# The transfers of five weight sums in one row, two more heap slots, and low halves that let other vector work pass: a hybrid decoder layer on one core

## The chip, the cores and the metric

The kernel runs on one core of one Trainium2 chip. The metric is the time of one execution in microseconds (us) of the device. Below, PE is TensorE (matmuls), DVE is VectorE, ACT is ScalarE, POOL is GpSimd, and SP is the engine that issues most DMA transfers.

## The reference

One decoder layer over 512 tokens of width 1024, in float32:

```python
u = rmsnorm(h, g_mix)
proj = u @ w_in                     # 1024 x 9232: all that follows is cut from it
ro = retention_chunkwise(rq, rk, rv)            # 8 heads, chunks of 128
y_ret = (silu(rgate) * groupnorm(ro)) @ w_ret_br
do = gated_delta_chunkwise(cq, ck, cv, g, beta) # 8 heads: a triangular solve per chunk,
                                                # then a scan over the 4 chunks
y_dn = (rmsnorm(do) * silu(dz)) @ w_dn_br
h = h + (sigmoid(gate_r) * y_ret + sigmoid(gate_d) * y_dn) @ w_o
up = causal_dwconv(rmsnorm(h) @ w_up) + b       # 1024 -> 2 x 2816
h = h + (silu(a) * b) @ w_down
out = rmsnorm(h)
```

## The kernel before

**Exact products from rounded halves.** Each weight block (128 x 1024 float32, 512 KB) is fetched by an SP transfer into a buffer `wraw` (four of them), rounded by ACT into `whi`, and what is left over is computed by DVE as `wlo = wraw - whi` (four buffers of each). PE multiplies three times per block: high by high, high by low, low by high. One task, `weights()` (line 334), does this for one block after the other. Only when it has issued the `wlo` does it let `fetch()` (line 272) issue the load of another block into the freed buffer.

**Seven products in place of eight.** Five square matrices (numbers 0 to 3: the two gates and the two branches; `OUT`: `w_o`) and `w_down` are multiplied by a scheme of seven half-size products. Four of the seven weight operands are sums of quarters of the matrix (`s1` to `s4`). These sums aren't computed by an engine: `presum()` (line 299) issues transfers on POOL's queue from DRAM to DRAM, a plain copy of one quarter (`s<-wm`) and then a transfer that adds another onto it (`s<-wm` or `s<-s`), eight of 1 MB for each of the five matrices. `presums()` (line 322) spaces them by the program's own clock, and ahead of each it puts a tiny ACT copy `tick` and a tiny POOL copy `tock`, so that POOL can't run ahead of the others.

**Stages, in order of time.** Input norm; the fronts of four delta heads and the retention projections (to about 190 us); the triangular solves, the scans of heads 0 to 3 and the fronts of heads 4 to 7, all mixed (to about 340 us); the gates' projections `pz`, the second solve and scans (to about 455 us); matrices 0 to 3 (tile `py`, to about 610 us; as matrix 3 begins, eight SP loads `h<-x` fetch the residual, line 1348); the OUT product (tile `po`, to about 663 us); the MLP's first product (`pa`, `pb`, to 910 us) and `w_down` (`pd`, to the end).

**How the order is set.** `body()` writes the program as generators that give way to each other. A class `Order` keeps a clock: each PE product advances it by a cost, and a task that is due by that clock is resumed between two products. Each engine then executes its own instructions strictly in the order that comes out, and waits where an operand isn't there. So a cost or a due time changes the order of every engine, and an instruction that waits holds up all behind it on its engine.

**The heap.** Nearly all tiles of 128 x 512 float32 (2 KB a partition) share one pool of `HEAP` slots. The allocator gives a new tile a slot whose earlier tile has no later reader in the program. Its first write then waits until that reader is done. In the scan stage head 4's key tiles, `A` and `ktok` (both written by ACT from the transposed keys `pkt`, `k_front`, line 767), thus stand in slots that heads 0 to 3 have used. A small pool holds the rest, among it the solve's scratch tile `xtmp` (`solve`, line 852) and the retention states `rS`.

Of the kernel before, what the change touches and what calls it, by code (L numbers as in the profile page):

```python
# [11 lines left out]
F32 = mybir.dt.float32  # L12
# [7 lines left out]
P = 128  # L20
# [4 lines left out]
H = 8  # L25
# [33 lines left out]
OUT, DOWN = 4, 5  # L59
# [38 lines left out]
class Order:  # L98
# [29 lines left out]
    def spawn(self, gen, after=0.0):  # L128
        self.n += 1
        heapq.heappush(self.tasks, ((self.clock if self.now is None else self.now) + after, self.n, gen))  # L130
# [91 lines left out]
def body(nc, tc, ctx, io):  # L222
    sp = nc.sync
    order = Order()
    spawn, poll, hold = order.spawn, order.poll, order.hold
    vec = Engine(order, "vec", nc.vector, vec_cost)
# [11 lines left out]
    small = mix.enter_context(tc.tile_pool(name="small", bufs=1))  # L238
    late = []

    HEAP, HEAP2, RAWB, WB = 61, 18, 4, 4

    def S(name, dt=F32):
        return heap.tile([P, T], dt, name=name, tag="s", bufs=HEAP)
# [7 lines left out]
    def PS(name):  # L252
        return psp.tile([P, T], F32, name=name, tag="ps")

    def v3(ap, n=4):
        return ap.rearrange("p (n f) -> p n f", n=n)
# [5 lines left out]
    def ck(n, f=P):  # L262
        return slice(n * f, (n + 1) * f)
# [35 lines left out]
    def presum(ss, parts):  # L299

        todo, late = [], []
        for s in ss:
            steps = [(s, name, i, q) for add in (1, 2) for name, *src in SUMS for i in range(parts) for q in (src[add - 1],)]
            steps = [(*x, n >= len(steps) // 2) for n, x in enumerate(steps)]
            todo += steps[:2 * parts] + late + steps[2 * parts:-parts]
            late = steps[-parts:]
        for s, name, i, q, add in todo + late:
            c = ck(i, 512 * INNER[s] // parts)  # L310
            kw = dict(accum_op=ALU.add) if add else {}
            pool.dma_start(sums[s, name][:, c], quarter(s, q)[:, c], max_dma_last_dim=2048, **kw)
            if add and i == parts - 1:
                made.add((s, name))
            yield
# [5 lines left out]
        act.copy(tick, ones[:, :1])  # L321
        pool.tensor_scalar(tock, tick, 1.0, None, ALU.mult)

    def presums(ss, parts, *times):

        todo = presum(ss, parts)
        for start, end, n in times:
            for i in range(n):
                while order.clock < start + (end - start) * i / n:
                    yield 0.5  # L330
                pace()
                if next(todo, 0) == 0:
                    return
                yield

    def weights():
        i = count["split"]
        if i == len(BLOCKS):
            return
        count["split"] += 1  # L340
        while i not in raws:
            yield 0.3
        raw = raws.pop(i)
        n = raw.shape[1]
        hi = wp.tile([P, n], F32R, name="whi", tag="whi", bufs=WB)
        act.copy(hi, raw)
        yield
        lo = wp.tile([P, n], F32R, name="wlo", tag="wlo", bufs=WB)
        vec.tensor_tensor(lo, raw, hi.bitcast(F32), ALU.subtract)
        ready[i] = (hi, lo)  # L350
        yield
        free[0] += 1
        fetch()
# [10 lines left out]
    def used():  # L364
        spawn(weights(), 0.1)
# [380 lines left out]
    GH = 4  # L746
    NS = GH * NT
    NP = 4 * NS
# [8 lines left out]

    spawn(clear(), 30.0)

    spawn(presums(range(3), 1, (110.0, 318.0, 23), (330.0, 330.0, 1)), 30.0)  # L760
    a_dram = [dram.tile([4, GH, NT, 32, 32], F32, name=f"a_dram{g}") for g in range(2)]
    x_dram = [dram.tile([4, GH, NT, 32, 32], F32, name=f"x_dram{g}") for g in range(2)]
    R32 = [ck(b, 32) for b in range(4)]
    heads = [dict(h=h, got=set()) for h in range(H)]
# [91 lines left out]
    def solve(g):  # L856

        group = heads[g * GH:(g + 1) * GH]
        while not all("k" in hd["got"] for hd in group):
            yield 0.3  # L860
        while g > 0 and not all("o" in hd["got"] for hd in heads[(g - 1) * GH:g * GH]):
            yield 0.3
        sa = [heap.tile([P, 32, 16], F32, name=f"sa{i}", tag="s", bufs=HEAP) for i in range(2)]
        adv = a_dram[g].rearrange("b h n i j -> (b h n) i j")
        for i in range(2):
            sp.dma_start(sa[i][:NP], adv[:, :, ck(i, 16)])
        xx = small.tile([P, 32, 32], F32, name="xx", tag="xx", bufs=1)
        tmp = small.tile([P, 32, 32], F32, name="xtmp", tag="xtmp", bufs=1)
        pool.memset(xx[:NP], 0.0)
        pool.memset(xx.rearrange("p a b -> p (a b)")[:NP, ::33], 1.0)  # L870
        yield 8.0
        for j in range(31):
            shp = [NP, j + 1, 31 - j]
            a = sa[j // 16][:NP, j + 1:, j % 16].unsqueeze(1).to_broadcast(shp)
            tv, xv_ = tmp[:NP, :j + 1, j + 1:], xx[:NP, :j + 1, j + 1:]
            vec.tensor_tensor(tv, a, xx[:NP, :j + 1, j:j + 1].to_broadcast(shp), ALU.mult)
            vec.tensor_tensor(xv_, xv_, tv, ALU.subtract)
            yield
        sp.dma_start(x_dram[g].rearrange("b h n i j -> (b h n) (i j)"), xx[:NP].rearrange("p a b -> p (a b)"))
        for b in range(4):  # L880
            sp.dma_start(tt_all[R32[b], :, R32[b]], x_dram[g][b].rearrange("h n j i -> j (h n) i"))
        yield 13.5
        for i, hd in enumerate(group):
            spawn(solve_up(hd, i), i * 4.0)
# [171 lines left out]
    def ret_state(hp):  # L1056
        sts = states[hp] = [None]
        for n in range(NT - 1):
            pk = PS("pkv")[:, :P]
            for e, r in enumerate(E64):  # L1060
                vv = rv[n][hp // 2][:, ck(2 * hp % 4 + e)]
                pe.matmul(pk[r], krot[n][:, hp, r], vv, start=True, stop=True)
            yield
            st = small.tile([P, P], F32, name="rS", tag="rS", bufs=7)
            if n == 0:
                vec.tensor_copy(st, pk)
            else:
                vec.tensor_tensor(st, pk, sts[n], ALU.add)
            yield
            act.activation(st, st, AF.Identity, scale=gch[:, hp:hp + 1])  # L1070
            sts.append(st)
            yield
# [147 lines left out]
                yield gap  # L1220

    def late_sums():
        while "up" not in heads[H - 1]["got"]:
            yield 0.5
        c = order.clock
        yield from presums((3, OUT), 1, (c, c + 125.0, 15), (c + 140.0, c + 140.0, 1))

    for src, raw, x in ((roT, rr_, "r"), (doT, dd, "d")):
        if x == "d":
# [174 lines left out]
    product(1, o_get, HK, [[(full, C[t], True, o_into(t, 0, C[t], ALU.add, True))] for t in range(2)])  # L1404
    product(6, o_get, HK, [[(full, A[t], False, o_into(t, 1, A[t], ALU.subtract, True))] for t in range(2)], tail=2)
    u2 = (u2hi, u2lo)
    spawn(presums((DOWN,), 4, (order.clock, order.clock + 200.0, 32)))


    def ffn_conv(ps, ci):  # L1410
# [11 lines left out]
    f_raw, act_raw, parts = {}, {}, {}  # L1422
# [7 lines left out]
        parts[name, k] = hi, lo  # L1430

    def combine_f(k):
        y, z = S(f"y{k}"), (S2 if k < 9 else S)(f"z{k}")
        combine(f_raw, k, NK, y, z)
        act_raw["T3", k], act_raw["T1", k] = halves(y)
        act_raw["T2", k], act_raw["T4", k] = halves(z)
        act_raw["B21", k], act_raw["B22", k] = halves(f_raw.pop(k + NK))
        del f_raw[k]
# [195 lines left out]
```

## Time and profile before

| | |
|---|---|
| median of 3 runs | 1023.11 us (1022.1 to 1024.28) |
| profiled execution, its time | 1023.75 us |
| profiled execution, its span (first to last instruction) | 1022.0 us |
| PE busy | 992.4 us, 97% |
| DVE busy | 734.0 us, 72% |
| ACT busy | 535.2 us, 52% |
| POOL busy | 166.0 us, 16% |
| granted clock of TensorE, mean | 0.986 |
| moved by DMA | 189.29 MB |

The profiled execution's time is 1.75 us over its span, and 0.64 us over the median. A row of a timeline gives start, duration, engine, line, operation and `out<-in`; in brackets stands how long the engine sat idle before it, and what ended the wait. A row of waits gives the total, the count and the longest. A row of windows gives the length of a stretch, the busy time of PE, weight load (PEld), DVE, ACT and POOL, then the granted clock, the DMA share and GB/s.

### The profile page before, as it was taken

To read this page: it belongs to the slowest core of one execution; us is meant where nothing else is said; L and a number is where in the kernel's file an instruction comes from. 1 tells how busy PE (TensorE), PEld (TensorE's weight loads), DVE (VectorE), ACT (ScalarE), POOL (GpSimd) and SP (SyncE) were. 2 spreads that over 40 slices of the span, in tenths; PEclk is the share of its full clock that TensorE was granted. 3 is DMA by queue.
4 is the path that set the end of the run, shared out by engine and by line. 5 is a ranking of instruction groups with operands and counts; after the bars stand their busy time and mean duration, and the time that the engine had idled before them with its cause. 6 is when DMAs were issued, how large, how long until landed. Compare 5 with 4: busy or idle time off the path is not lost.

```text
span 1022.0 us, 14344 instructions
## 1 busy us (share of the span) xinstructions
PE 992.4 (97%) x5241; PEld 825.0 (81%) x5241; DVE 734.0 (72%) x1372; ACT 535.2 (52%) x1130; POOL 166.0 (16%) x212
## 2 busy tenths in 40 slices
PE   8999999979999999999999979999999999999997
PEld 7888888767778888888888767788888888888886
DVE  5867797545577796667699869966655676778785
ACT  5599222257744523467686455654444343356664
POOL 3021212112323200032211000022112221000001
PEclk8999999998999999999999989999999999999999
DMA  7243559655757754159999964655669999346663
GB/s 261 72 150 117 138 205 210 204 156 111 202 156 178 167 125 124 42 167 267 346 340 268 272 213 133 199 193 197 221 212 206 207 205 223 91 127 190 202 187 122
DMA packets 82230, 189.29 MB, mean 185 GB/s; under 512 B 22704, under 2 KB 31216, under 8 KB 82160
## 3 DMA queue, kind: packets, MB, share of 16 engines
q1 hardware_dynamic: 54640, 123.36, 37.0%
q0 software_dynamic: 27520, 65.02, 28.3%
q8 instruction: 41, 0.67, 0.2%
q14 instruction: 29, 0.24, 0.1%
HBM read 185.17 MB, written 68.19 MB: 248 GB/s over the span
## 4 chain that ended last, share of the span: by engine, by line
PE 84%; DVE 8%; DMA 3%; issue 2%; ACT 2%; POOL 0%; SPq 0%; POOLq 0%; ACTq 0%; DVEq 0%
PE pa L215 12%; PE pb L215 12%; PE pd L215 10%; PE py L215 9%; PE pz L215 9%; PE pr L215 9%; PE pk L215 5%; PE pv L215 4%; PE pq L215 4%; PE psc L215 3%; DVE wlo L200 2%; DVE res L200 2%; PE pm L215 2%; PE po L215 1%; PE pro L215 1%
## 5 line engine op out<-in xcount | busy, mean ns | idle before, releaser
L200 DVE TENSOR_TENSOR wlo<-wraw,whi 128x1024 fp32r<-128x1024 f32 x212 | 254.6, 1202 | 70.7 <-ACT whi L200 67.8
L200 ACT CAST whi<-wraw 128x1024 fp32r<-128x1024 f32 x212 | 219.0, 1035 | 163.4 <-PE pr L215 60.8
L200 POOL TENSOR_SCALAR tock<-tick 128x1 f32<-128x1 f32 x72 | 31.4, 436 | 461.5 <-ACT tick L200 461.4
L200 DVE SCALAR_TENSOR_TENSOR acc<-pb,prm,acc 128x511 f32<-128x511 f32 (+1 forms) x44 | 33.0, 750 | 57.1 <-ACT acc L200 56.4
L215 PE MATMUL pa<-u2hi,whi 128*128 128x512 f32 (+1 forms) x192 | 72.1, 375 | 1.1 <-ACT u2hi L200 1.1
L215 PE MATMUL pa<-u2lo,whi 128*128 128x512 f32 (+1 forms) x192 | 72.1, 376 | 0.8 <-DVE u2lo L200 0.8
L215 PE MATMUL pa<-u2hi,wlo 128*128 128x512 f32 (+1 forms) x192 | 71.9, 375 | 0.0
L215 PE MATMUL pb<-u2hi,whi 128*128 128x512 f32 (+1 forms) x184 | 70.0, 381 | 0.0
L215 PE MATMUL pb<-u2lo,whi 128*128 128x512 f32 (+1 forms) x184 | 69.9, 380 | 0.0
L215 PE MATMUL pb<-u2hi,wlo 128*128 128x512 f32 (+1 forms) x184 | 69.9, 380 | 0.0
L215 PE MATMUL py<-whi,oh 128*128 128x512 f32 x160 | 63.4, 396 | 0.0
L215 PE MATMUL py<-whi,ol 128*128 128x512 f32 x160 | 63.0, 394 | 0.0
L215 PE MATMUL py<-wlo,oh 128*128 128x512 f32 x160 | 62.9, 393 | 0.0
L215 PE MATMUL pd<-whi,T 128*128 128x512 f32 (+1 forms) x198 | 55.4, 366 | 0.0
L215 PE MATMUL pz<-uhi,whi 128*128 128x512 f32 x128 | 52.4, 409 | 0.0
L215 PE MATMUL pr<-whi,uhi 128*128 128x512 f32 x128 | 51.5, 402 | 0.0
L215 PE MATMUL pr<-whi,ulo 128*128 128x512 f32 x128 | 50.0, 391 | 0.0
L215 PE MATMUL pz<-uhi,wlo 128*128 128x512 f32 x128 | 50.0, 390 | 0.0
L215 PE MATMUL pz<-ulo,whi 128*128 128x512 f32 x128 | 49.9, 390 | 0.0
L215 PE MATMUL pr<-wlo,uhi 128*128 128x512 f32 x128 | 49.9, 390 | 0.0
L200 DVE SCALAR_TENSOR_TENSOR acc<-pa,prm,acc 128x511 f32<-128x511 f32 (+1 forms) x44 | 33.0, 750 | 19.0 <-ACT acc L200 18.2
L215 PEld LDWEIGHTS pa<-u2hi,whi 128*128 128x128 f32 x192 | 36.9, 192 | 7.6 <-ACT u2hi L200 1.4
(318 smaller groups left out, 2462.0 us busy)
## 6 DMA issues: line engine op xcount, KB each, us to landing
wraw<-w SPq DMA_DIRECT2D x100, 512.0 KB, 4.4
s<-wm POOLq DMA_DIRECT2D x30, 1024.0 KB, 7.6
wraw<-s SPq DMA_DIRECT2D x60, 512.0 KB, 4.3
s<-wd POOLq DMA_DIRECT2D x24, 704.0 KB, 5.3
wraw<-wm SPq DMA_DIRECT2D x30, 512.0 KB, 7.2
s<-s POOLq DMA_DIRECT2D x10, 1024.0 KB, 12.7
wraw<-wd SPq DMA_DIRECT2D x15, 512.0 KB, 3.7
s<-s POOLq DMA_DIRECT2D x8, 704.0 KB, 8.7
```

Source lines behind the costliest of these rows:

```text
L200: return f(out, *args, **kw)
L215: self.engine.matmul(out, lhsT, rhs, start=start, stop=stop, **kw)
```

## The change

Five edits.

1. One list of 40 transfers for all five matrices replaces a list for matrices 0 to 2 (24 of them, spread over clock 110 to 330) and one for 3 and OUT (16, from the end of head 7's solve over 125, and one at 140). Now 27 go between clock 110 and 322, four between 336 and 360, and the last nine from the end of head 4's solve over 68, and one at 85.
2. `weights()` pauses between the high and the low half: while DVE's planned work reaches over 0.8 us ahead, the low half is put off by 0.3 us, at most 12 times.
3. The solve's scratch tile shrinks from 4 KB to 1 KB a partition (its columns are now packed), the retention states have 6 buffers for 7.
4. The space gives two more heap slots (63 for 61). The second heap, used from matrix 1 on, has 16 for 18.
5. Seven of the MLP's `z` tiles in place of nine lie in the second heap.

```diff
-    HEAP, HEAP2, RAWB, WB = 61, 18, 4, 4
+    HEAP, HEAP2, RAWB, WB = 63, 16, 4, 4
...
-    def presums(ss, parts, *times):
-
-        todo = presum(ss, parts)
+    def presums(todo, *times):
+
         for start, end, n in times:
             for i in range(n):
                 while order.clock < start + (end - start) * i / n:
...
         act.copy(hi, raw)
         yield
+
+        n_ = 0
+        while order.free.get("vec", 0.0) > order.now + 0.8 and n_ < 12:
+            n_ += 1
+            yield 0.3
         lo = wp.tile([P, n], F32R, name="wlo", tag="wlo", bufs=WB)
         vec.tensor_tensor(lo, raw, hi.bitcast(F32), ALU.subtract)
...
-    spawn(presums(range(3), 1, (110.0, 318.0, 23), (330.0, 330.0, 1)), 30.0)
+    todo = presum((0, 1, 2, 3, OUT), 1)
+    spawn(presums(todo, (110.0, 322.0, 27), (336.0, 360.0, 4)), 30.0)
...
-        tmp = small.tile([P, 32, 32], F32, name="xtmp", tag="xtmp", bufs=1)
+        tmp = small.tile([P, 256], F32, name="xtmp", tag="xtmp", bufs=1)
...
-            tv, xv_ = tmp[:NP, :j + 1, j + 1:], xx[:NP, :j + 1, j + 1:]
+            tv, xv_ = v3(tmp[:NP, :(j + 1) * (31 - j)], j + 1), xx[:NP, :j + 1, j + 1:]
...
-            st = small.tile([P, P], F32, name="rS", tag="rS", bufs=7)
+            st = small.tile([P, P], F32, name="rS", tag="rS", bufs=6)
...
     def late_sums():
-        while "up" not in heads[H - 1]["got"]:
+        while "up" not in heads[GH]["got"]:
             yield 0.5
         c = order.clock
-        yield from presums((3, OUT), 1, (c, c + 125.0, 15), (c + 140.0, c + 140.0, 1))
+        yield from presums(todo, (c, c + 68.0, 8), (c + 85.0, c + 85.0, 1))
...
-    spawn(presums((DOWN,), 4, (order.clock, order.clock + 200.0, 32)))
+    spawn(presums(presum((DOWN,), 4), (order.clock, order.clock + 200.0, 32)))
...
-        y, z = S(f"y{k}"), (S2 if k < 9 else S)(f"z{k}")
+        y, z = S(f"y{k}"), (S2 if k < 7 else S)(f"z{k}")
```

Three places in the order are moved that the prediction speaks of.

**ACT in the scans.** `A4` and `ktok4` are head 4's tiles, `vn` and `o` are steps of the scans of heads 0 to 3 (`psc` is their PSUM tile), `gb4` is head 4's decay tile. Before:

```order
L200 ACTIVATE gb4_2293<-gb4_2293 128x512
L200 COPY vn_2344<-psc_2302 128x128
L200 ACTIVATE A4_2348,ssk_2350<-pkt_2324 128x128 x4
L200 ACTIVATE ktok4_2349<-pkt_2324,ekd_175 128x128 x4
L200 ACTIVATE o0_2079<-psc_2237,rqs_722 128x128
L200 ACTIVATE junk_2361,ssqo_2080<-o0_2079 128x128
L200 COPY vn_2368<-psc_2280 128x128
L200 COPY vn_2372<-psc_2310 128x128
```

And now:

```order
L200 ACTIVATE A4_2273,ssk_2275<-pkt_2249 128x128 x4
L200 ACTIVATE ktok4_2274<-pkt_2249,ekd_175 128x128 x4
L200 COPY vn_2302<-psc_2295 128x128
L200 COPY vn_2307<-psc_2271 128x128
L200 COPY vn_2311<-psc_2284 128x128
L200 COPY tt_178<-pm3_2313 64x4x64
L200 COPY tick_2343<-ones_104 128x1
```

Head 4's eight instructions still stand ahead of the `vn` of the scans, but one scan step earlier, ahead of `gb4` rather than behind it. In the built program the slots are other ones: before, `A4` follows head 0's keys `k0` in its slot and `ktok4` follows head 0's `vtok0`, both still read by head 0's last scan step; now `A4` follows a scratch tile `m1` of a finished solve step and `ktok4` follows `A2`, which the solve has left.

**SP as matrix 3 begins.** `wraw<-s2_3` and so on are weight blocks of matrix 3's sums, `h1` the residual. Before:

```order
L282 DMA wraw_5831<-s2_3_91 128x1024
L282 DMA wraw_5856<-s2_3_91 128x1024
L282 DMA wraw_5914<-s1_3_89 128x1024
L1348 DMA h1_00_5872<-x 128x512
L1348 DMA h1_01_5874<-x 128x512
L1348 DMA h1_10_5876<-x 128x512
L1348 DMA h1_11_5878<-x 128x512
L1348 DMA h1_20_5880<-x 128x512
L1348 DMA h1_21_5882<-x 128x512
L1348 DMA h1_30_5884<-x 128x512
L1348 DMA h1_31_5886<-x 128x512
L282 DMA wraw_5941<-s1_3_89 128x1024
```

And now:

```order
L282 DMA wraw_5836<-s2_3_91 128x1024
L1353 DMA h1_00_5873<-x 128x512
L1353 DMA h1_01_5875<-x 128x512
L1353 DMA h1_10_5877<-x 128x512
L1353 DMA h1_11_5879<-x 128x512
L1353 DMA h1_20_5881<-x 128x512
L1353 DMA h1_21_5883<-x 128x512
L1353 DMA h1_30_5885<-x 128x512
L1353 DMA h1_31_5887<-x 128x512
L282 DMA wraw_5909<-s2_3_91 128x1024
L282 DMA wraw_5934<-s1_3_89 128x1024
```

The eight residual loads have moved ahead of two weight blocks.

**DVE in the OUT product.** `mT2`, `mT4`, `mT1` and `mB21` are low halves of the data operands (made from `mt` and `mr`), `wlo` are low halves of weights; `wraw_6195` is in both programs the first block of the product by `mT2`, `wraw_6222` the second. Before:

```order
L200 TENSOR_TENSOR mT2_6307<-mt2_6301,mT2_6306 128x512
L200 TENSOR_TENSOR wlo_6324<-wraw_6195,whi_6313 128x1024
L200 TENSOR_TENSOR mB21_6337<-mr01_6326,mB21_6336 128x512
L200 TENSOR_TENSOR h1_00_5872<-h1_00_5872,po_6263 128x512
L200 SCALAR_TENSOR_TENSOR mt4_6358<-mt2_6292,mr01_6326 128x512
L200 TENSOR_TENSOR mB21_6348<-mr11_6339,mB21_6347 128x512
L200 TENSOR_TENSOR h1_10_5876<-h1_10_5876,po_6264 128x512
L200 SCALAR_TENSOR_TENSOR mt4_6371<-mt2_6301,mr11_6339 128x512
L200 TENSOR_TENSOR wlo_6376<-wraw_6222,whi_6355 128x1024
```

And now:

```order
L200 TENSOR_TENSOR wlo_6332<-wraw_6181,whi_6266 128x1024
L200 SCALAR_TENSOR_TENSOR mt4_6339<-mt2_6288,mr01_6304 128x512
L200 TENSOR_TENSOR mB21_6324<-mr01_6304,mB21_6323 128x512
L200 TENSOR_TENSOR h1_00_5873<-h1_00_5873,po_6261 128x512
L200 TENSOR_TENSOR mT4_6342<-mt4_6339,mT4_6341 128x512
L200 TENSOR_TENSOR mB21_6349<-mr11_6334,mB21_6348 128x512
L200 TENSOR_TENSOR h1_10_5877<-h1_10_5877,po_6262 128x512
L200 SCALAR_TENSOR_TENSOR mt4_6365<-mt2_6308,mr11_6334 128x512
L200 TENSOR_TENSOR mt1_6373<-mr00_6020,mr20_6271 128x512
L200 TENSOR_TENSOR mT4_6371<-mt4_6365,mT4_6370 128x512
L200 TENSOR_TENSOR wlo_6382<-wraw_6195,whi_6321 128x1024
```

The low half of `wraw_6195` stood right behind `mT2`; now the low half of the block before it stands there, and nine other instructions come between the two.

## The prediction

> **What bounds the kernel now.** I read the page first, then PE's waits, then the windows around them. PE is the bound:
>
> ```profile
> PE 992.4 (97%) x5241; PEld 825.0 (81%) x5241; DVE 734.0 (72%) x1372; ACT 535.2 (52%) x1130; POOL 166.0 (16%) x212
> PE pmt L219 <- DVE res L200: 6.5, 1, 6.5
> PE psc L215 <- ACT vn L200: 6.5, 1, 6.5
> PE po L215 <- DVE mT L200: 2.2, 2, 1.2
> 692.97 5.44 PE pa L215 x24
> ```
>
> The change leaves PE's 5241 matmuls as they are, so it can only win idle time and clock. There are two large waits, one among the scans (`psc`) and one in matrix 3 (`pmt`). Undisturbed, 24 matmuls of 512 columns take 5.44 us, 0.227 each. The windows (length, PE, PEld, DVE, ACT, POOL busy, then the clock) show that each wait is paid twice:
>
> ```profile
> 224.40:230.80 6.40, 0.00 (x0) 0.00 (x0) 2.14 (x10) 3.12 (x17) 1.68 (x2) 0.88 0.05 8
> 230.80:236.00 5.20, 5.16 (x22) 4.51 (x23) 1.34 (x4) 2.55 (x11) 0.00 (x0) 0.50 0.02 3
> 586.80:593.30 6.50, 0.03 (x1) 0.00 (x0) 2.52 (x4) 3.36 (x5) 0.00 (x0) 0.83 0.88 327
> 593.30:597.00 3.70, 3.64 (x11) 3.06 (x12) 3.52 (x5) 2.80 (x5) 0.00 (x0) 0.50 0.73 259
> 597.00:600.00 3.00, 3.00 (x13) 2.46 (x12) 0.22 (x1) 1.05 (x1) 0.00 (x0) 0.84 0.58 183
> ```
>
> After the first wait PE runs 5.2 us at clock 0.50, which loses 2.6; after the second, 3.7 at 0.50 and 3.0 at 0.84, which loses 1.85 + 0.48 = 2.3. The waits themselves are 6.47 and 6.53 (rows below). So the first is worth 9.1 us and the second 8.8.
>
> **The scan wait.** These rows, from the timelines of PE, ACT, DVE and POOL, are one chain:
>
> ```profile
> 224.40 0.28 ACT L200 ACTIVATE A<-pkt 128x128 f32<-128x128 f32 x1 [4.20 <-PE psc L215]
> 225.58 0.17 DVE L200 TENSOR_SCALAR ssk<-ssk 128x4 f32<-128x4 f32 x1 [4.97 <-ACT A L200]
> 225.83 1.04 POOL L200 TENSOR_TENSOR rk<-ssk,mhalf 128x4 f32<-128x4 f32 x1 [7.78 <-DVE ssk L200]
> 228.42 0.34 DVE L200 SCALAR_TENSOR_TENSOR R<-psc,c,vtok 128x128 f32<-128x128 f32 x1
> 228.79 1.15 ACT L200 ACTIVATE ktok<-pkt,ekd 128x128 f32<-128x128 f32 x4 [3.25 <-DVE R L200]
> 230.54 0.41 ACT L200 COPY vn<-psc 128x128 f32<-128x128 f32 x2
> 230.84 0.58 PE L215 MATMUL psc<-vn,ktok 128*128 128x128 f32 x1 [6.47 <-ACT vn L200]
> ```
>
> ACT's `A` reads `pkt`, but what released it is a scan matmul: `A4` waits for its slot, whose last reader is head 0's scan. Then DVE and POOL finish `A`, only then comes DVE's `R`, the last reader of `vtok0`, in whose slot `ktok4` stands; and behind `ktok4` on ACT stand the two `vn` for which PE waits. In the order of the change the pair stands a scan step earlier, in slots whose tiles were last read in the step before (`m1`, `A2`), and the three `vn` behind it wait for nothing of head 4. So both links are gone: **-9.1 us**. What was pushed out goes to others: `k0`'s slot now takes the load `egb4` on SP, `vtok0`'s the tile `q4` on ACT, `q0`'s the tile `o3`. Behind `egb4` on SP stand head 4's `A` transfers, `gb5` and one weight block; a block has four buffers' time, and ACT's `q4` and `o3` follow readers that no longer hang on ACT's own queue. I cost these at nothing; if that cover is gone, the price is the first rival's.
>
> **The matrix 3 wait.** Timelines of POOL, SP, ACT, DVE and PE:
>
> ```profile
> 435.73 0.80 POOL L200 DMA_DIRECT2D s<-wm  x1
> 572.57 0.32 SPq L282 DMA_DIRECT2D wraw<-s  x1
> 572.94 3.87 SPq L1348 DMA_DIRECT2D h<-x  x8
> 574.35 1.27 POOL L200 DMA_DIRECT2D s<-s  x1 [0.36 <-issue]
> 576.94 15.38 SPq L282 DMA_DIRECT2D wraw<-s  x5
> 589.67 1.04 ACT L200 CAST whi<-wraw 128x1024 fp32r<-128x1024 f32 x1 [10.63 <-DMA wraw<-s]
> 590.75 1.23 DVE L200 TENSOR_TENSOR wlo<-wraw,whi 128x1024 fp32r<-128x1024 f32 x1 [7.80 <-ACT whi L200]
> 591.89 1.41 DVE L200 TENSOR_TENSOR res<-res,res 128x512 f32<-128x512 f32 x2
> 593.36 0.90 PE L219 MATMUL pmt<-cst,res 128*128 128x128 f32 x3 [6.53 <-DVE res L200]
> wraw<-s SPq DMA_DIRECT2D x60, 512.0 KB, 4.3
> ```
>
> Eight residual loads (2 MB) and the last sum transfer are in flight together; the weight block issued at 576.94 lands 12.7 us later, where the median is 4.3. ACT and DVE wait for it, and `res`, which PE needs, stands on DVE behind the low half that waits. The change takes away both partners. Sixteen sums went from 435.7 (first row), where head 7's solve ends, to 574. Now the last nine begin where head 4's ends, earlier, and take 85 us of the program's clock: the last is issued by 435.7 + 85 = 521, 50 us before matrix 3. And SP issues the residual two blocks earlier, right behind the first `wraw<-s`. DVE in this stretch has no slack to show:
>
> ```profile
> 564.85 1.22 DVE L200 TENSOR_TENSOR wlo<-wraw,whi 128x1024 fp32r<-128x1024 f32 x1
> 565.98 0.69 DVE L200 TENSOR_TENSOR ol<-rz,oh 128x512 fp32r<-128x512 f32 x1
> 560.00:580.00 20.00, 20.00 (x90) 16.57 (x89) 19.88 (x27) 13.09 (x18) 1.48 (x2) 1.00 0.90 276
> ```
>
> From one start to the next a low half takes 1.13, another tile 0.60 to 0.64. On before's time scale the first `wraw<-s` load was free at 566.1, as the low half of 564.85 ended, so the residual now goes from 566.4 instead of 572.9. The next block waits for the low half of an earlier one, now eight tiles behind 565.98: 565.98 + 8 x 0.6 + 1.2 = 572.0. If it lands in 4.3 to 8.0 us its low half is done by 579 to 582.5; PE comes to it about 583 (the waiting `pmt`, due at 586.8, stands some 17 matmuls behind). So the wait goes: **-8.8**. The put-off low halves cost something here: by the same count the two ahead end at 572.0 and 575.0, where PE wants them at 571.5 and 574.2: **+0.8**.
>
> **The OUT product.** DVE is full here too, with PE waiting 1.2 and 1.0:
>
> ```profile
> 605.23 1.23 DVE L200 TENSOR_TENSOR wlo<-wraw,whi 128x1024 fp32r<-128x1024 f32 x1 [1.50 <-ACT whi L200]
> 637.55 1.46 DVE L200 TENSOR_TENSOR mT<-mt,mT 128x512 fp32r<-128x512 f32 x2
> 620.00:640.00 20.00, 19.03 (x90) 15.47 (x89) 19.44 (x29) 11.24 (x17) 0.00 (x0) 1.00 0.42 132
> ```
>
> Before, from the row at 605.23 to the end of the first `mT` at 638.2, DVE does 9 low halves and 35 tiles: 33.0 us, so (33.0 - 9 x 1.13) / 35 = 0.65 a tile. In the new order PE waits earlier, in the third matmul of the `mT2` product, for the low half of `wraw_6195`. Up to there DVE has 7 low halves and 33 tiles, 29.4 us, plus two gaps of 0.7 where `mT2` now directly follows the `mt2` that ACT must copy in between: done at 636.0. PE would be there 23 matmuls before the 637.1 of its old wait, at 631.9. So 4.1 us of wait in one place, and about 0.7 one block on, for 2.2 before: **+2.6**. Bounds: nothing, if PE comes later or the tiles interleave better, and 4.3 with the clock.
>
> For the clock, the row first: 2.0 us without matmuls at 664 to 666.2 were enough.
>
> ```profile
> 664.00:666.00 2.00, 0.39 (x2) 0.19 (x1) 2.00 (x9) 2.00 (x9) 0.00 (x0) 1.00 0.73 262
> 666.00:668.00 2.00, 1.65 (x7) 1.65 (x8) 2.00 (x6) 2.00 (x6) 1.96 (x3) 0.55 0.28 36
> 668.00:670.00 2.00, 2.00 (x13) 2.00 (x12) 2.00 (x8) 0.61 (x3) 1.82 (x3) 0.59 0.79 305
> ```
>
> The two stretches at 0.55 and 0.59 lose 1.7 us. The Trainium skill (TensorE: Matmul & The Clock Gate, part 1) says that the clock halves after about 3.4 us of idling, in a window that runs freely. By that rule a wait of 4.1 in one piece would halve it; waits of 1 us, as before here, would not, and the latter the trace shows.
>
> **The rest.** More transfers fall in 110 to 360 us: 27 in 212 us for 24 in 220. Weight loads there have room:
>
> ```profile
> DMA to landing us min/median/max: 3.3/4.4/8.8
> DMA to landing us min/median/max: 3.2/8.0/13.1
> ```
>
> Between 100 and 400 us (first row) even 8.8 + 1.04 + 1.23 = 11.1 us lies within four buffers' 4 x 5.44 us: nothing. On POOL's queue, a `s<-s` that adds onto an unfinished sum would hold up the reciprocal roots behind it; the four at 336 to 360 stand where few are due: nothing. The packed scratch tile does the same elements, the sixth `rS` buffer has steps to spare, and the second heap's two slots move to the first: nothing.
>
> **The sum.** 1023.75 - 9.1 - 8.8 + 0.8 + 2.6 = 1009.25 for the profiled execution. That stood 0.64 over the median: **1008.6 us**.
>
> **Rivals.**
> 1. *The scan wait re-forms* in another slot (`egb4`, `q4`, `o3`, each written right after its old tile's last read). For it: those three gaps are as tight as the old two. Against: no reader stands behind them on the same queue. 1008.6 + 9.1 = 1017.7.
> 2. *The load still comes late*, as two more blocks now stand behind the residual. For it: a landing of 12.7 would put the low half at 587.0, 3.4 us past PE's 583.6, and with 2 of clock gives 1014.0. Against: without the sum, with 6.5 us more of lead, that landing has no cause.
> 3. *The OUT wait halves the clock*: 1008.6 + 1.7 = 1010.3, by the rows at 666 to 670, or the skill's rule.
> 4. *Both waits stay* in other shapes: 1008.6 + 9.1 + 5.4 = 1023.1, no change: the new slots and the new list would do nothing.
> 5. *Slower: low halves starve the weight ring.* A buffer is freed only behind its low half. Between 540 and 600 us a block takes 8.0 (second row above) + 1.04 + 1.23 = 10.3 for four buffers, 2.57 each, and PE needs one in 12 matmuls, 2.72. Put off by the full 12 x 0.3 = 3.6 us it is 3.47, 0.75 too slow. Over some 59 blocks (500 to 660 us) that is up to 44 us, 1052.6. It decides from (1023.1 - 1008.6) / 59 = 0.25 a block, a mean delay of 1.6 us. Against: with the sums out of the way the landing falls towards 4.3, which covers even the full delay (10.2 / 4 = 2.5).
>
> **How the numbers follow.** Forecast 0.58, rival 3 0.08, rival 2 0.11, rival 1 0.11, rival 4 0.05, rival 5 0.07. About 0.2% (2 us) is what a measurement can tell from no change. Faster: 0.58 + 0.08 + 0.11 + 0.11 = 0.88; same 0.05; slower 0.07. The range reaches up to rival 1, 1018. Down, OUT could cost nothing and lose its old 2.2 as well (1008.6 - 2.6 - 2.2 = 1003.8), matrix 3's 0.8 not appear, and the idle remnants of the scans go too:
>
> ```profile
> 240.00:260.00 20.00, 19.45 (x134) 15.47 (x133) 13.02 (x44) 16.60 (x49) 7.51 (x9) 1.00 0.82 167
> 280.00:300.00 20.00, 19.75 (x112) 15.28 (x112) 14.91 (x47) 9.19 (x26) 6.72 (x9) 1.00 0.71 196
> ```
>
> 0.55 + 0.25: 1002.2, so 1002.
>
> **What would show it.** Right: PE's waits have neither `psc <- vn` nor `pmt <- res` over 2 us; the clock is 1.00 from 215 to 240 and in the stretch of matrix 3; no `s` transfer is issued after 521 us; the residual goes ahead of the second `wraw<-s`; PE's longest wait between the input norm and the MLP is for a `wlo` in `po`, 3 to 5 us. Wrong: a clock of 0.5 anywhere before OUT, ACT waits of over 5 us for `wraw`, or `wlo` waits spread over matrices 1 to 3.

## The result and the profile after

| | before | after |
|---|---|---|
| median | 1022.61 us (1021.47 to 1024.28, 4 runs) | 1007.05 us (1005.87 to 1009.29, 4 runs) |
| profiled execution, its span | 1022.0 us | 1005.0 us |
| PE busy | 992.4 us, 97% | 985.0 us, 98% |

The ratio of the medians is 0.985, with a 95% interval from 0.983 to 0.987: faster by 15.6 us, where 14.5 were forecast. PE's longest waits over the whole changed kernel (total, count, longest):

```profile
PE po L215 <- DVE wlo L200: 3.7, 1, 3.7
PE pt L219 <- DVE xs L200: 2.5, 2, 1.7
PE pa L215 <- DVE u2lo L200: 2.3, 2, 1.6
PE psc L215 <- ACT vn L200: 0.4, 1, 0.4
```

Both waits of 6.5 us are gone: `psc` is at 0.4 and `pmt` isn't in the list. The new first row is the wait that the prediction named for the OUT product. The windows of the changed kernel (length, busy time of PE, PEld, DVE, ACT, POOL, then the granted clock) around the scans, matrix 3 and OUT:

```profile
215.00:240.00 25.00, 24.59 (x185) 20.57 (x184) 14.35 (x52) 19.23 (x64) 9.59 (x12) 1.00 0.96 197
571.00:600.00 29.00, 29.00 (x141) 24.04 (x140) 23.79 (x31) 17.38 (x23) 0.00 (x0) 1.00 0.51 169
612.00:618.00 6.00, 3.35 (x8) 2.67 (x9) 5.23 (x8) 3.74 (x5) 0.00 (x0) 0.59 0.28 87
618.00:620.00 2.00, 2.00 (x7) 1.55 (x6) 2.00 (x4) 1.10 (x2) 0.00 (x0) 0.54 0.36 61
```

In these windows of the scans and of matrix 3 the clock is at 1.00, and PE isn't idle at all from 571 to 600. In OUT the clock is down to 0.5 behind the new wait. On SP's queue the residual goes right behind the first `wraw<-s`; on POOL's the last sum had gone out 60 us earlier (timelines, and ACT's on the block behind):

```profile
551.96 0.33 SPq L282 DMA_DIRECT2D wraw<-s  x1
552.34 3.97 SPq L1353 DMA_DIRECT2D h<-x  x8
558.10 15.18 SPq L282 DMA_DIRECT2D wraw<-s  x7
491.69 1.28 POOL L200 DMA_DIRECT2D s<-s  x1
563.25 1.05 ACT L200 CAST whi<-wraw 128x1024 fp32r<-128x1024 f32 x1 [1.61 <-DMA wraw<-s]
```

The block of 558.10 is on ACT at 563.25, 5.1 us after its issue; before it was 12.7.

Where the time went is read most simply from the first matmul of each stage. These groups of PE (count, ns shortest/median/longest, first and last start) are of the changed kernel:

```profile
L215 PE MATMUL pr<-whi,uhi x128: 389/389/500, 98.8 to 191.4; 128*128 128x512 f32 x128
L215 PE MATMUL pz<-uhi,whi x128: 389/389/504, 326.7 to 441.1; 128*128 128x512 f32 x128
L215 PE MATMUL py<-whi,oh x160: 389/389/481, 454.0 to 596.7; 128*128 128x512 f32 x160
L215 PE MATMUL pa<-u2hi,whi x192: 278/389/390, 647.3 to 887.2; 128*128 128x512 f32 x160, 128*128 128x256 f32 x32
L215 PE MATMUL pd<-whi,T x198: 277/389/397, 923.3 to 998.3; 128*128 128x512 f32 x154, 128*128 128x256 f32 x44
```

The differences of these starts give the length of each stage. From the same groups of every kernel, in us:

| kernel | to `pr` | `pr` to `pz` (scans) | `pz` to `py` | `py` to `pa` (matrices, OUT) | `pa` to `pd` (MLP) | to the end |
|---|---|---|---|---|---|---|
| before | 100.6 | 238.5 | 127.4 | 198.6 | 275.2 | 81.7 |
| after | 98.8 | 227.9 | 127.3 | 193.3 | 276.0 | 81.7 |
| slots alone | 99.2 | 229.2 | 127.4 | 190.9 | 275.2 | 81.7 |
| slots alone, second run | 98.9 | 230.0 | 127.4 | 199.5 | 275.2 | 81.7 |
| slots and list | 98.8 | 230.1 | 127.4 | 190.2 | 274.5 | 81.7 |
| slots and low halves | 100.7 | 227.7 | 127.2 | 200.1 | 275.9 | 81.7 |
| last sum earlier | 98.9 | 238.9 | 128.3 | 195.5 | 274.5 | 81.7 |
| residual earlier | 98.8 | 242.8 | 127.5 | 195.9 | 274.5 | 81.7 |
| sums denser | 98.7 | 238.7 | 127.4 | 191.9 | 274.6 | 81.7 |
| eight of OUT's let off | 98.6 | 227.7 | 127.4 | 188.4 | 274.9 | 81.7 |
| low halves only early | 98.9 | 228.1 | 127.4 | 189.7 | 274.5 | 81.7 |
| one of OUT's let off | 99.3 | 227.9 | 127.4 | 193.5 | 277.0 | 81.7 |

From before to after: -1.8 at the start (where the clock was at 0.50 before, see the last section), -10.6 in the scans, -0.1, -5.3 in matrices and OUT, +0.8 in the MLP: -17.0, the difference of the two spans.

### The profile page after: what moved, and what is told of

It is laid out like the page before. It is cut to its first block, busy times and chain, and to the rows that moved or that the text cites. A ratio compares the mean times of both kernels' runs of the same rounds, so it can differ in the third digit from the quotient of the medians.

```text
span 1005.0 us, 14343 instructions
## 1 busy us (share of the span) xinstructions
PE 985.0 (98%) x5241; PEld 819.9 (82%) x5241; DVE 732.5 (73%) x1372; ACT 538.8 (54%) x1134; POOL 173.1 (17%) x212
## 4 chain that ended last, share of the span: by engine, by line
PE 89%; DVE 4%; ACT 2%; issue 2%; DMA 1%; POOL 1%; SPq 0%; POOLq 0%; DVEq 0%
PE py L215 14%; PE pa L215 12%; PE pb L215 12%; PE pd L215 10%; PE pz L215 9%; PE pr L215 9%; PE pk L215 4%; PE pq L215 4%; PE pv L215 4%; PE po L215 3%; PE psc L215 3%; PE pm L215 1%; PE pro L215 1%; DVE wlo L200 1%; DMA gb<-g_dram 1%
## 5 line engine op out<-in xcount | busy, mean ns | idle before, releaser
L200 POOL TENSOR_SCALAR tock<-tick 128x1 f32<-128x1 f32 x72 | 34.8, 484 | 395.3 <-ACT tick L200 395.3
L215 PEld LDWEIGHTS pa<-u2lo,whi 128*128 128x128 f32 x192 | 36.1, 188 | 9.0 <-DVE u2lo L200 2.7
```

The lines of the kernel that those rows point to most:

```text
L200: return f(out, *args, **kw)
L215: self.engine.matmul(out, lhsT, rhs, start=start, stop=stop, **kw)
```

## The experiments

The theory is the prediction's: the new slots take away the scan wait; the list, by parting sum and residual, the matrix 3 wait; and the standing back costs time in OUT. The rivals give the same gains to another of the three edits, or to one of the two transfers alone.

### The scans: the slots alone

Before, with only the slots changed:

```diff
-    HEAP, HEAP2, RAWB, WB = 61, 18, 4, 4
+    HEAP, HEAP2, RAWB, WB = 63, 16, 4, 4
...
-        tmp = small.tile([P, 32, 32], F32, name="xtmp", tag="xtmp", bufs=1)
+        tmp = small.tile([P, 256], F32, name="xtmp", tag="xtmp", bufs=1)
...
-            st = small.tile([P, P], F32, name="rS", tag="rS", bufs=7)
+            st = small.tile([P, P], F32, name="rS", tag="rS", bufs=6)
...
-        y, z = S(f"y{k}"), (S2 if k < 9 else S)(f"z{k}")
+        y, z = S(f"y{k}"), (S2 if k < 7 else S)(f"z{k}")
```

> Before, with only the two more heap slots, the compact scratch tile and the sixth rS buffer; the list of sums and the low halves as before. Theory (the scan wait hung on the slots of A4 and ktok4 alone): psc <- vn goes, the clock in 215 to 240 us is 1.00, the matrix 3 wait for res stays at about 6.5 us with its slow clock behind it, and the time is 1022.6 - 9.1 = 1013.5 us. Rival (the sums, which leave the stretch at another time, or the low halves freed the scans): the 6.5 us at psc stay and the time is 1022.6. Rival (the slots change both): the time is near 1005.

Measured: 1013.67 us (1005.35 to 1016.77, 6 runs) against 1022.81; ratio 0.990, interval 0.987 to 0.993. No `psc` wait is left, and the scan stage takes 229.2 us for 238.5. ACT's timeline there:

```profile
217.92 0.63 ACT L200 ACTIVATE gb<-gb 128x512 f32<-128x512 f32 x1
218.60 0.28 ACT L200 ACTIVATE A<-pkt 128x128 f32<-128x128 f32 x1
219.62 1.17 ACT L200 ACTIVATE ktok<-pkt,ekd 128x128 f32<-128x128 f32 x4
```

Head 4's pair still stands behind `gb` here, as before the change, and neither half of it waits any more. So it is the slots and not the pair's earlier place in ACT's order. Which of this edit's four parts did it isn't shown.

The medians differ by 9.1, the theory's figure, but that it agrees to the tenth is luck, for one run stands far from the others: the profiled one took 1005.35, the five others 1011.2 to 1016.8, and its profile has hardly a wait in matrix 3. So the same kernel ran once more.

> The kernel with the slots alone once more, for a second look: its first profile took 1005.35 us, with the last sum issued 6.0 us behind the residual and 0.9 us of wait for res, while its five other runs took 1011.2 to 1016.8. Theory (what separates the runs is how far the sum and the residual overlap): the time is 1011 to 1017 and the wait for res 3 to 7 us, with the sum issued within 4 us of the residual or a block behind it landing in 10 us or more. Rival (the runs differ elsewhere, in the scans or at the start): the wait for res is again under 1.5 us whatever the time.

Measured: 1014.4 us (one run). From the timelines, first of the earlier profile, then of this one: SP's residual, POOL's last sum, ACT on the block behind them, and PE's wait.

```profile
561.82 3.74 SPq L1348 DMA_DIRECT2D h<-x  x8
567.86 1.27 POOL L200 DMA_DIRECT2D s<-s  x1
573.36 1.05 ACT L200 CAST whi<-wraw 128x1024 fp32r<-128x1024 f32 x1 [5.00 <-DMA wraw<-s]
577.04 0.66 PE L219 MATMUL pmt<-cst,res 128*128 128x128 f32 x4 [0.89 <-DVE res L200]
```

```profile
563.32 3.84 SPq L1348 DMA_DIRECT2D h<-x  x8
564.17 1.28 POOL L200 DMA_DIRECT2D s<-s  x1
580.32 1.04 ACT L200 CAST whi<-wraw 128x1024 fp32r<-128x1024 f32 x1 [11.45 <-DMA wraw<-s]
584.00 1.11 PE L219 MATMUL pmt<-cst,res 128*128 128x128 f32 x4 [7.34 <-DVE res L200]
```

One program, and the wait for `res` is 0.9 or 7.3 us, as the sum starts 6.0 or 0.85 us behind the residual. The stages differ by 8.6 us in matrices and OUT (190.9, 199.5) and by under 1 elsewhere. So the slots cure the scans; and the wait in matrix 3 comes and goes in one unchanged program, with the time between the starts of the two transfers. The other five timed runs have no profile, so how far the two overlapped there isn't known.

### Matrix 3: the list without the low halves, and the low halves without the list

The changed kernel without the pause in `weights()`:

```diff
-        n_ = 0
-        while order.free.get("vec", 0.0) > order.now + 0.8 and n_ < 12:
-            n_ += 1
-            yield 0.3
```

> The changed kernel without the standing back of the low halves; slots and list of sums as changed. Theory (matrix 3 waited because the last sum and the residual were in flight together): no psc <- vn wait; the residual goes one block later than in the changed kernel, as before, but alone, its follower lands in about 8 us instead of 12.7 and the wait for res is under 2 us; OUT has its two waits of about 1.1 us for mT again and clock 1.00. Time 1007.05 - 3.4 (what OUT cost more in the changed kernel) + 0 to 1.5 = 1003.6 to 1005.2 us. Rival (the low halves' place on DVE was what cured matrix 3): the wait for res stays at 5 to 6.5 us with its clock and the time is 1012 to 1013.

Measured: 1006.08 us (1004.37 to 1008.59, 4 runs), ratio 0.984 (0.982 to 0.986). Among PE's waits from the scans to OUT (total, count, longest), the one for `res` is at 0.2 us:

```profile
PE psc L215 <- DVE R L200: 1.6, 1, 1.6
PE po L215 <- DVE mT L200: 2.2, 2, 1.3
PE pmt L219 <- DVE res L200: 0.2, 1, 0.2
```

The block behind the residual took 7.9 to 8.3 us to land, as the theory had it for the residual alone, and that is early enough. So list and slots together give the whole of the gain: from slots alone to slots and list the median falls by 7.6 us, the stage of a run with the wait from 199.5 to 190.2. The time missed the upper end of the expectation by 0.9, for a reason that it didn't have: without the standing back a wait of 1.6 for `R` comes up in the scans (230.1 for 227.9). Against the changed kernel the intervals of the two ratios overlap, so no worth of the standing back as a whole was measured; by the stages of the two profiles it gives 2.2 in the scans and takes 3.1 in matrices and OUT and 1.5 in the MLP.

The other way round, the changed kernel with the old lists of sums:

```diff
-    todo = presum((0, 1, 2, 3, OUT), 1)
-    spawn(presums(todo, (110.0, 322.0, 27), (336.0, 360.0, 4)), 30.0)
+    spawn(presums(range(3), 1, (110.0, 318.0, 23), (330.0, 330.0, 1)), 30.0)
...
-        while "up" not in heads[GH]["got"]:
+        while "up" not in heads[H - 1]["got"]:
...
-        yield from presums(todo, (c, c + 68.0, 8), (c + 85.0, c + 85.0, 1))
+        yield from presums((3, OUT), 1, (c, c + 125.0, 15), (c + 140.0, c + 140.0, 1))
```

> The changed kernel with the old lists of sums: the last sum goes out at about 562 us, some 10 us behind the residual. Theory (the two have to be in flight together): scan wait gone, the residual has landed when the sum starts, the loads of matrix 3 land in 4 to 9 us and PE waits there under 1.5 us in all: 1007 to 1009 us. Rival (the sum alone delays the loads): a load behind it lands in 10 us or more and PE waits 3 to 6 us for a wlo or a res in matrix 3, 1011 to 1015 us. Rival (without the list the scan wait is back): 1016.

Measured: 1014.3 us (1012.89 to 1015.66, 6 runs), ratio 0.992 (0.990 to 0.994): the price of the first rival, but not by its reason. I had expected the sum 10 us behind the residual; it came 4.6 us behind, so the two did overlap, by the timelines of SP, POOL, ACT and PE:

```profile
557.58 3.81 SPq L1353 DMA_DIRECT2D h<-x  x8
562.17 1.27 POOL L200 DMA_DIRECT2D s<-s  x1 [0.36 <-issue]
571.95 1.04 ACT L200 CAST whi<-wraw 128x1024 fp32r<-128x1024 f32 x1 [8.70 <-DMA wraw<-s]
573.54 0.50 PE L215 MATMUL py<-whi,oh 128*128 128x512 f32 x1 [2.15 <-ACT res L200]
```

The window behind that wait:

```profile
574.00:577.00 3.00, 3.00 (x9) 2.33 (x8) 1.47 (x3) 1.04 (x1) 0.00 (x0) 0.50 1.06 358
```

The block lands after 8.7 us, hardly later than with the residual alone (7.9 to 8.3 without the standing back, where PE waited 0.2). Here ACT waits 8.70 for it, a `res` that PE needs stands behind it on ACT, and the clock halves. So this run doesn't show by the landing that the overlap costs. What it does show: the new order of the low halves doesn't do without the list. The list is worth 7.2 us with the low halves (1014.3 to 1007.05) and 7.6 without.

### Which of the two transfers

Three edits in the order of before, where the scan wait stays. First the last sum due 21 us of the program's clock earlier; the fifteen transfers ahead of it are also drawn together, from 125 to 119 us:

```diff
-        yield from presums((3, OUT), 1, (c, c + 125.0, 15), (c + 140.0, c + 140.0, 1))
+        yield from presums((3, OUT), 1, (c, c + 119.0, 15), (c + 119.0, c + 119.0, 1))
```

> Before, with one number changed: the last sum of the late list is due 119 us after head 7's solve instead of 140, so about 21 us ahead of the residual. Slots and low halves as before. Theory (sum and residual together): the block behind the residual lands in 7 to 8.5 us, the matrix 3 wait shrinks from 6.5 to 0 to 2 us and its slow clock goes; the scan wait stays. 1022.6 - 8.8 + 0 to 2 = 1013.8 to 1015.8 us. Rival (the residual's eight loads alone make the block late): no change, 1022.6.

Measured: 1019.5 us (1017.65 to 1023.45, 12 runs), ratio 0.998 (0.996 to 0.999). Neither expectation. POOL's and SP's rows say why:

```profile
567.70 1.27 POOL L200 DMA_DIRECT2D s<-s  x1 [12.35 <-DMA s<-s]
574.75 7.12 SPq L1348 DMA_DIRECT2D h<-x  x8
```

The last sum reads the one before it, whose transfer took 17.3 us. So the edit moved the due time by 21 us and the transfer by some 8 against the residual: it began 7.0 us ahead of it, not 1.4 behind, and ran across it, from 567.70 to 581.2. The blocks behind the residual, counted from their own issue, landed early:

```profile
DMA to landing us min/median/max: 5.9/6.5/7.0
```

That figure misleads, for SP issued them late: the eight residual loads took 7.12 us to go out (last section). PE still waits 1.8 and 2.7 us for `res`, at a clock of 1.00. So the whole late list was made denser, with the last two sums far enough apart:

```diff
-        yield from presums((3, OUT), 1, (c, c + 125.0, 15), (c + 140.0, c + 140.0, 1))
+        yield from presums((3, OUT), 1, (c, c + 105.0, 15), (c + 118.0, c + 118.0, 1))
```

> Before, with the whole late list faster: its 15 transfers spread over 105 us instead of 125 and the last due at 118 instead of 140, so that the last sum, which waits for the one ahead of it (some 18 us), can start at about 554 and end ahead of the residual of 572.9. Theory (the two together): the residual is alone, the block behind it lands in about 8 us as in the run without the standing back (8.0), the wait for res is under 2 us: 1014 to 1016 us. Rival (the residual alone suffices): landing over 11, wait 5 to 6.5, 1021 to 1023. Should the sums, 7 us apart instead of 8.3, delay the blocks of matrices 1 and 2, waits appear between 470 and 560 us.

Measured: 1015.59 us (1014.58 to 1018.54, 6 runs), ratio 0.994 (0.992 to 0.996), as the theory had it. The timelines of POOL, SP, ACT and PE:

```profile
556.37 1.27 POOL L200 DMA_DIRECT2D s<-s  x1 [4.87 <-DMA s<-s]
570.98 3.85 SPq L1348 DMA_DIRECT2D h<-x  x8
583.42 1.05 ACT L200 CAST whi<-wraw 128x1024 fp32r<-128x1024 f32 x1 [6.04 <-DMA wraw<-s]
587.11 0.66 PE L219 MATMUL pmt<-cst,res 128*128 128x128 f32 x4 [1.94 <-DVE res L200]
```

The sum (12.2 us long) is over at 568.6; with the residual alone, the blocks behind it land after 8.4 to 8.7 us, and PE waits 1.9 us, with the clock at 1.00 behind it. Matrices and OUT take 191.9 for 198.6. No slot and no low half was touched here: the timing of the sums alone takes the second wait from 6.5 to 1.9 us, and its slow clock. Last, the residual a matrix earlier, the sum left where it was:

```diff
-        if s == 3:
+        if s == 2:
             for t in range(NT):
                 for i in range(2):
                     h1[t][i] = S(f"h1_{t}{i}")
                     sp.dma_start(h1[t][i], xv[t, :, ck(i, T)])
```

> Before, with only the residual's eight loads issued one matrix earlier (ahead of matrix 2); the last sum stays where matrix 3's first blocks are loaded. The earlier run that moved the last sum forward didn't part the two: that sum waited 12.35 us for the one ahead of it and ran from 567.7. Theory (sum and residual together make the block 12.7 us late): with the sum alone the block of that place lands in at most 8.5 us, the wait for res is 0 to 2 us, the scan wait stays: 1022.8 - 8.8 + 0 to 2 = 1014.0 to 1016.0 us. Rival (the sum alone makes the block late): landing 11 us or more, the wait stays at 5 to 6.5 us: 1021 to 1023. A new wait in matrix 2, where the residual now stands in front of blocks while other sums run, would show as a wait for res or wlo some 40 us earlier.

Measured: 1021.9 us (1020.33 to 1024.32, 12 runs), ratio 1.000 (0.999 to 1.002). In matrix 3, with the sum alone, the blocks land after at most 9.0 us (not 11 or more, the rival's), and the waits for `res` fall from 6.5 to 3.0 with the clock at 1.00. But at its new place the residual meets other transfers of the list, the plain copy of 528.75 and the adding one of 537.27 (timelines of SP, POOL, ACT and PE):

```profile
531.88 6.57 SPq L1348 DMA_DIRECT2D h<-x  x8
528.75 0.78 POOL L200 DMA_DIRECT2D s<-wm  x1
537.27 1.32 POOL L200 DMA_DIRECT2D s<-wm  x1
547.54 1.05 ACT L200 CAST whi<-wraw 128x1024 fp32r<-128x1024 f32 x1 [5.41 <-DMA wraw<-s]
564.12 0.50 PE L215 MATMUL py<-whi,oh 128*128 128x512 f32 x1 [1.59 <-ACT res L200]
```

And two of PE's waits over the whole kernel:

```profile
PE pmt L219 <- DVE res L200: 3.0, 2, 2.7
PE pm L215 <- DMA tt<-x_dram: 2.5, 2, 2.0
```

Blocks issued between 538.6 and 539.9 land after 8.9 to 12.2 us, but PE waits only 0.3 us right behind them. Its wait of 1.59 at 564.12 follows a block issued at 554.27 that took 8.2 us, beside two adding transfers, when the residual had long landed. Matrices and OUT are 2.7 us shorter by the landmarks (195.9); the scan stage of this profile is 4.3 longer, 2.5 of it the wait for `tt` in the solve, ahead of all that was moved. Why the median gives nothing of the 2.7 stays open.

Together, counted from SP's first residual load to the landing of the first block behind the eight, so that what SP holds back is in it:

| kernel | the sum began | us |
|---|---|---|
| slots and list | long before | 12.0 |
| sums denser | 14.6 us ahead, and had ended | 12.3 |
| last sum earlier | 7.0 us ahead | 13.4 |
| slots alone, second run | 0.85 us behind | 16.9 |
| before | 1.4 us behind | 16.6 |
| slots and low halves | 4.6 us behind | 14.3 |
| slots alone | 6.0 us behind | 11.4 |

The two large figures, and the two waits of 6.5 and 7.3 us, belong to the two cases in which the sum began within 1.5 us behind the residual. An overlap as such does less: it is in the rows of 7.0 ahead, 4.6 and 6.0 behind too (and of the 14.3, 1.8 passed between the issue of the last residual load and that of the block).

### OUT: which low halves cost the time

The changed kernel, with OUT's first eight low halves let off:

```diff
-        while order.free.get("vec", 0.0) > order.now + 0.8 and n_ < 12:
+        while order.free.get("vec", 0.0) > order.now + 0.8 and n_ < 12 and not 0 <= i - BLOCKS.index(next(b for b in BLOCKS if b[:2] == ("q", OUT))) < 8:
```

> The changed kernel, but the low halves of OUT's first eight blocks don't stand back. Theory (the standing back of one low half there is the 3.7 us wait, and that wait is why the clock fell): no wait for wlo in po over 1 us, two waits for mT of about 1.1 as before the change, clock 1.00 in 600 to 620, 1007.05 - 3.0 = 1004.0 us (pmt to pa took 75.6 us in the changed kernel and 72.6 without any standing back). Rival (DVE is simply full there, the wait moves to the next low half): a wait of 2 to 4 us for a later wlo or mT and 1006 to 1008.

Measured: 1001.06 us (1000.46 to 1001.07, 5 runs), ratio 0.980 (0.978 to 0.982): faster than before and than the changed kernel, and the best of all. The wait is gone, and so is the slow clock. What is left of PE's waits in `po`, and a window:

```profile
PE po L215 <- DVE mT L200: 1.7, 3, 0.8
```

```profile
600.00:620.00 20.00, 18.95 (x86) 14.89 (x84) 19.02 (x27) 11.51 (x17) 0.00 (x0) 1.00 0.39 128
```

It is worth 4.9 us in matrices and OUT (193.3 to 188.4) and 1.1 in the MLP, twice the 3.0 expected. So in OUT the standing back of these eight cost 4.9, not the 3.1 by which the kernel without any of it is shorter; 3.7 of wait and 2.6 of slow clock (worked out below), less the 1.7 that PE now waits for `mT`, make 4.6 of it. Then with only the low half for which PE waited let off:

```diff
-        while order.free.get("vec", 0.0) > order.now + 0.8 and n_ < 12:
+        while order.free.get("vec", 0.0) > order.now + 0.8 and n_ < 12 and i != BLOCKS.index(next(b for b in BLOCKS if b[:2] == ("q", OUT))) + 4:
```

> The changed kernel, but one low half doesn't stand back: that of OUT's fifth block (wraw_6195), whose place on DVE moves nine tiles forward, about 9 x 0.65 = 5.9 us. Theory (this one low half is the 3.7 us wait, and that wait is why the clock fell to 0.50 behind it): no wlo wait over 1 us in OUT, clock 1.00, pmt to pa in 71 to 72.5 us instead of 75.6: 1002.5 to 1004 us. Rival (the others of the first eight low halves matter as much, since exempting eight gave 1001.06): waits of 1 to 2.5 us for a wlo or mT remain and the time is 1004.5 to 1006.5.

Measured: 1008.48 us (1007.05 to 1009.49, 6 runs), ratio 0.986 (0.984 to 0.989). The theory falls, and the rival's mechanism holds, with a larger size than it had (the time lies above both forecasts): the wait comes at the next block, 4.3 us later and nearly as long, again with the clock at 0.50 behind it:

```profile
618.96 0.50 PE L215 MATMUL po<-wlo,mT 128*128 128x512 f32 x1 [3.59 <-DVE wlo L200]
```

```profile
620.00:622.00 2.00, 2.00 (x6) 1.52 (x6) 2.00 (x3) 0.00 (x0) 0.00 (x0) 0.50 0.74 252
```

So it is not one instruction's place but DVE's backlog: between the low halves that end at 609.6 and the next, at 617.69, DVE does twelve other tiles here, and PE stands for that next one. At last the standing back only in the first quarter of the blocks:

```diff
-        while order.free.get("vec", 0.0) > order.now + 0.8 and n_ < 12:
+        while order.free.get("vec", 0.0) > order.now + 0.8 and n_ < 12 and i < len(BLOCKS) // 4:
```

> The changed kernel, with the low halves standing back only in the first quarter of the weight blocks (the input norm to the scans), and not in the matrices, OUT and the MLP. Theory (the standing back helps the scans by 2.2 us, costs 3.0 in OUT and 1.5 in the MLP, by the landmarks of the changed kernel and of the one without any): no psc wait over 0.5, OUT's waits two of 1.1, and 1007.05 - 3.0 - 1.5 = 1002.6 us. Rival (the back half's order has little to do with it): 1005 to 1007.

Measured: 1002.36 us (1001.28 to 1003.64, 4 runs), ratio 0.981 (0.979 to 0.983); the theory had 1002.6. The scans keep their gain (228.1), matrices and OUT take 189.7, the MLP 274.5, with OUT's two waits for `mT` at 2.2 us in all, as before the change.

## Why the prediction was right

**The scan wait, -9.1.** Right in place, cause and size: the slots alone gave 9.3 and 8.5 by the stage in the two profiles. (The 9.1 of the medians has matrix 3's changing wait in it.) The pair's earlier place in ACT's order, which the prediction named beside the slots, wasn't needed. The stage gained 10.6 after the change. The rest came from the low halves (230.1 to 227.9), which the prediction had cost at nothing there.

**The matrix 3 wait, -8.8.** Right in cause, a little large in size: with slots and list the stage is 8.4 shorter than before, with the denser sums alone 6.7 (6.6 by the medians), where 1.9 of wait stays. The whole wait with its slow clock came where the sum began just behind the residual; the residual alone left 0.2 to 1.9 us of wait, the sum alone 3.0. That SP issues the residual two blocks earlier wasn't needed for it: without the standing back it goes one block later and PE waits 0.2.

**The low halves in matrix 3, +0.8.** Didn't come. From the first `py` to the first `pmt` it is 117.7 us for 117.6, and PE was busy 29.00 of 29.00 us behind. Either PE's need or DVE's end was off by at least that; no run shows which.

**The OUT product, +2.6.** Right in mechanism, too small in size. The wait is at the low half and the matmul that were named (the third of the `mT2` product, at 614.65), 3.69 for the forecast 4.1. The 0.7 one block on didn't come, but the clock fell: from 614.65 to about 620 PE ran at half speed, (618 - 614.65) x 0.5 + 2.00 x 0.46 = 2.6 lost. In the terms of the prediction that is 3.69 + 2.6 - 2.2 = 4.1 for its 2.6. It is rival 3, put at 8 in 100. The step that was wrong is the choice to leave the clock out of the sum at a forecast wait of 4.1 us, though rows of before showed it falling where PE had next to nothing for 2.0. The Trainium skill (TensorE: Matmul & The Clock Gate, part 1) says that the clock halves after about 3.4 us of idling. Behind the 3.69 us here it did; but it also did behind a wait of 2.15, so the rule isn't the whole (below).

**The rest, nothing.** The MLP cost 0.8. Kernels whose low halves stand back there take 274.9 to 277.0 for it, the others 274.5 to 275.2, so it was probably the low halves. No wait of PE's in the scans is over 0.4, so the slots of `egb4`, `q4` and `o3` cost it nothing (rival 1), the residual's follower landed in 5.1 us (rival 2), the weight ring didn't starve (rival 5): between 520 and 590 us its blocks landed in 3.9 us at the median.

```profile
DMA to landing us min/median/max: 3.2/3.9/5.1
```

**The sum.** Forecast were -9.1 in the scans and -8.8 + 0.8 + 2.6 = -5.4 in matrices and OUT; measured -10.6 and -5.3, then +0.8 in the MLP, and -1.8 at the start, which is none of the change's. The total is right by its two large terms. That it is within 1.6 us owes something to errors that cancel: the clock in OUT and the MLP's 0.8 against the gain of the low halves in the scans and the 0.8 in matrix 3 that wasn't paid.

## What to carry to other kernels

When a load comes late, ask what else was in flight with it, and which began first: here two transfers that alone cost PE 0.2 to 3 us of wait cost 6.5 and 7.3 where one began just behind the other, and in one program some 5 us between their starts made the difference. A due time moves an instruction only as far as what it depends on lets it. And an edit that lets less urgent work pass has to be costed stage by stage: the same rule gained 2 us in the scans and lost 5 in OUT, where DVE is full. Letting eight low halves off was worth another 6 us, keeping the rule to the first quarter of the blocks 4.7.

## What the runs showed of the hardware

**The length of a wait alone doesn't decide the clock.** PE stood still for 2.15 us in the kernel with slots and low halves, and the clock was 0.50 within half a microsecond behind it (the row at 574.00 above). Behind 2.73 us with the residual earlier, and 2.69 with the last sum earlier, it stayed at 1.00:

```profile
595.00:600.00 5.00, 4.69 (x23) 3.97 (x24) 3.93 (x6) 4.91 (x8) 0.00 (x0) 1.00 0.72 246
```

```profile
592.00:596.00 4.00, 4.00 (x20) 3.40 (x21) 3.36 (x4) 3.50 (x6) 0.00 (x0) 1.00 0.72 253
```

Of these waits, those of 3.59 us and more halved it, the one of 2.15 did too, and so did two of 1.13 and 0.84 close together (before, the prediction's rows from 664 on); those of 1.94, 2.69 and 2.73 did not. So behind a wait of up to 3 us it is a matter of when it falls, or of what PE did around it; which, no run tells.

**The first microseconds differ from run to run.** Where the clock was 0.50 from 12 to 16 us (before, and slots with low halves), `pr` began at 100.6 and 100.7; in the other executions at 98.6 to 99.3. In the same two PE's first wait for `xs`, at about 8.5 us, was 2.2 and 2.3 us long, in the others 0.4 to 1.7. That is 1.8 us between the profiles of before and after, and none of the change's, for the changed kernel with the old lists has it too. Their windows, before first:

```profile
12.00:16.00 4.00, 3.87 (x19) 2.99 (x18) 3.41 (x9) 2.75 (x8) 0.00 (x0) 0.50 1.04 397
```

```profile
12.00:16.00 4.00, 3.73 (x32) 3.45 (x33) 4.00 (x11) 3.64 (x11) 0.00 (x0) 1.00 1.04 408
```

**SP never had more than eight transfers in flight.** Of SP's 307 transfers in each of the twelve traces, none was issued before the eighth ahead of it had landed. So where earlier ones land late, SP holds back the next: with the last sum earlier, the seventh residual load went out at 579.37, as a block issued at 570.84 landed (8.5 us, beside the sum), and the eight took 7.12 us to issue. With the residual earlier they took 6.57; in the other runs 3.7 to 4.1. Whether the chip or the program sets the eight, no run shows.
